# A one-core block of scans, long convolutions and expert retrieval: how the routing looks up the sixteen chosen keys of a pair

## The chip, the cores and the metric

The kernel runs on one core of a Trainium2 chip. The metric is the device time of one execution in microseconds (us). Engines are called as in the profile: PE multiplies matrices (PEld loads its weights), DVE, ACT and POOL are the vector, scalar and GpSimd engines, SP issues transfers.

## The reference

One trunk layer over 1024 latent tokens of width 1024, with a context of 256 tokens: an input projection, two parallel mixers (a state-space scan in both directions and a gated long convolution), an output projection, then a retrieval over 128 x 128 single-neuron experts. The change touches the retrieval only:

```python
q = (hb @ wq).reshape(PEER_BLOCK, PEER_HEADS, 2, PEER_DKEY // 2)
s = jnp.einsum('thsd,snd->thsn', q, subkeys).astype(jnp.float32)
s1, i1 = lax.top_k(s[:, :, 0], PEER_TOPK)
s2, i2 = lax.top_k(s[:, :, 1], PEER_TOPK)
cand = (s1[..., :, None] + s2[..., None, :]).reshape(PEER_BLOCK, PEER_HEADS, PEER_TOPK * PEER_TOPK)
sc, ci = lax.top_k(cand, PEER_TOPK)
e1 = jnp.take_along_axis(i1, ci // PEER_TOPK, axis=-1)
e2 = jnp.take_along_axis(i2, ci % PEER_TOPK, axis=-1)
idx = e1 * PEER_KEYS + e2
gate = jax.nn.softmax(sc, axis=-1).astype(hb.dtype)
```

For every token and each of 8 heads, the 16 best of 128 keys are found on either side, then the 16 best pairs. `take_along_axis` turns a pair's two ranks (0 to 15) into its two key numbers (0 to 127). The experts' rows are then weighted with the gates.

## The kernel before

The tokens lie in 8 blocks of 128, one token to a partition. Blocks 5 to 7 gather their experts' rows by number (class `Experts`, `gathered`: indirect transfers that POOL issues, L1511, with a DVE dot product, L1535, or a weighted sum, L1548, for each row). Blocks 0 to 4 are done densely: the scores of all 128 groups of 128 experts are computed by PE (`score`, L1634), multiplied by a table of gates, and sent through PE again (`down`, L1674). The dense table of gates comes from `Route.spread`.

Routing (`peer`, class `Route`) has these parts:

- `firsts`, `first`: PE multiplies the tokens with merged key matrices (`qacc`, L1368), ACT copies the scores out (`r_sc`, L1370), and DVE finds the top 16 of 128 by MAX8, FIND_INDEX8 and MATCH_REPLACE8 (`top16`, L1344 to L1348).
- `second(b)`, the function that changes: for one block it adds the candidate pairs (L1396, L1398), finds the top 16 of 112 for each head, splits the position of a pair into two ranks (L1410 to L1418), and looks the ranks up. The lookup is made twice, t = 0 and 1 for the two sides. A one-hot tile `r_oh` of 128 x (8 heads x 16 pairs x 16 ranks) is written by a comparison of each pair's rank with 0 to 15 (L1423), multiplied by the 16 key numbers of the head (L1425), and summed over ranks by one reduction (L1427). ACT makes the key numbers (`r_if`, L1393) for both sides in one 128x256 activation. Softmax of the gates follows (L1431 to L1436).
- `spread(b)`, for blocks 0 to 4: one-hot rows e0 and e2 by DVE (L1457, L1459), e0 times the gate split between POOL (three of eight tokens, L1461) and ACT (five, L1463), products by PE (L1467), copied out by ACT (L1469) and stored.

Which runs beside which is written in `peer` with the generators `both` and `chain`: `second(5)` beside the firsts of blocks 6 and 7, `second(6)` and `second(7)` beside the firsts of blocks 0 to 4, `second(0)` after these, and `second(b + 1)` beside `spread(b)`. At each step `Experts.beside` adds 48 score tiles in all and some of the gathered rows. How many of these are done before the last stage is counted in steps, not in time. Within this, a scheduler with a model of the engines sets the order of instructions on each engine. Every engine runs its own list in order.

The last stage (`pour`, `run`), after routing, works off the remaining scores, the down products and the remaining rows.

Of the kernel before, what the change touches and what calls it, by code (L numbers as in the profile page):

```python
# [12 lines left out]
BF16 = mybir.dt.bfloat16  # L13
I32 = mybir.dt.int32
U32 = mybir.dt.uint32
AF = mybir.ActivationFunctionType
ALU = mybir.AluOpType
AX = mybir.AxisListType
# [1272 lines left out]
class Route:  # L1291
# [9 lines left out]
    def tables(self, mid):  # L1301
        nc = self.K.nc
        it = mid.tile([128, 128], I32, name="iota_i")
        nc.gpsimd.iota(it, pattern=[[1, 128]], base=0, channel_multiplier=0)
        self.iota = mid.tile([128, 128], F32, name="iota_f")
        nc.vector.tensor_copy(self.iota, it)
        self.val = mid.tile([128, NB, 16, 16], F32, name="r_val")
        self.idx = mid.tile([128, NB, 16, 16], U32, name="r_idx")

# [76 lines left out]
    def second(self, b, wk):  # L1386


        K, nc = self.K, self.K.nc
        V = nc.vector  # L1390
        val = self.val[:, b]
        idf = wk.tile([128, 16, 16], BF16, name="r_if", bufs=1)
        nc.scalar.activation(idf, self.idx[:, b], AF.Copy)  # L1393
        cand = wk.tile([128, 8, 112], F32, name="r_cand", bufs=1)
        v1, v2 = val[:, 0:16:2], val[:, 1:16:2]
        V.tensor_add(cand[:, :, :64].rearrange("p h (i j) -> p h i j", j=16),  # L1396
                     v1[:, :, 0:4, None].to_broadcast([128, 8, 4, 16]), v2[:, :, None, :].to_broadcast([128, 8, 4, 16]))
        V.tensor_add(cand[:, :, 64:].rearrange("p h (i j) -> p h i j", j=4),  # L1398
                     v1[:, :, 4:16, None].to_broadcast([128, 8, 12, 4]), v2[:, :, None, 0:4].to_broadcast([128, 8, 12, 4]))
        s = wk.tile([128, 8, 16], F32, name="r_s", bufs=2)  # L1400
        ci = wk.tile([128, 8, 16], U32, name="r_ci", bufs=2)
        tmp2 = wk.tile([128, 112], F32, name="r_tmp2", bufs=2)
        for h in range(8):
            self.top16(s[:, h], ci[:, h], cand[:, h], tmp2)
            if h % 2:
                yield
        pos = wk.tile([128, 4, 8, 16], U32, name="r_pos", bufs=1)
        for j, (n, op) in enumerate(((4, ALU.logical_shift_right), (15, ALU.bitwise_and),
                                     (2, ALU.logical_shift_right), (3, ALU.bitwise_and))):
            V.tensor_scalar(pos[:, j], ci, n, None, op0=op)  # L1410
        pof = wk.tile([128, 4, 8, 16], F32, name="r_pof", bufs=1)
        nc.scalar.activation(pof, pos, AF.Copy)
        up = wk.tile([128, 8, 16], F32, name="r_up", bufs=1)
        V.tensor_scalar(up, pof[:, 0], 4.0, None, op0=ALU.is_ge)
        V.scalar_tensor_tensor(pof[:, 2], pof[:, 2], 12.0, pof[:, 0], op0=ALU.subtract, op1=ALU.subtract)
        V.tensor_sub(pof[:, 3], pof[:, 3], pof[:, 1])
        V.tensor_mul(pof[:, 2:4], pof[:, 2:4], up[:, None].to_broadcast([128, 2, 8, 16]))
        V.tensor_add(pof[:, 0:2], pof[:, 0:2], pof[:, 2:4])  # L1418
        e = wk.tile([128, 2, 8, 16], F32, name="r_e", bufs=2)
        for t in range(2):  # L1420
            oh = wk.tile([128, 8, 16, 16], BF16, name="r_oh", bufs=2)
            ohv = oh.rearrange("p h k j -> p (h k) j")
            V.tensor_tensor(ohv, pof[:, t].rearrange("p h k -> p (h k)")[:, :, None].to_broadcast([128, 128, 16]),  # L1423
                                    self.iota[:, None, :16].to_broadcast([128, 128, 16]), op=ALU.is_equal)
            V.tensor_mul(oh, oh, idf[:, t:16:2, None, :].to_broadcast([128, 8, 16, 16]))  # L1425
            yield
            V.tensor_reduce(e[:, t].rearrange("p h k -> p (h k)"), ohv, axis=AX.X, op=ALU.add)  # L1427
        ef = e.rearrange("p t h k -> p t (h k)")
        g = self.gate[b] if b >= ND else wk.tile([128, 128], F32, name="r_g", bufs=2)
        gv = g.rearrange("p (h k) -> p h k", k=16)  # L1430
        V.tensor_sub(gv, s, s[:, :, 0:1].to_broadcast([128, 8, 16]))  # L1431
        nc.scalar.activation(g, g, AF.Exp)
        sm = wk.tile([128, 8], F32, name="r_sm", bufs=1)
        V.tensor_reduce(sm, gv, axis=AX.X, op=ALU.add)
        V.reciprocal(sm, sm)
        V.tensor_mul(gv, gv, sm[:, :, None].to_broadcast([128, 8, 16]))  # L1436
        if b >= ND:
            V.scalar_tensor_tensor(self.ids[b], ef[:, 0], 128.0, ef[:, 1], op0=ALU.mult, op1=ALU.add)
        self.found = ef, g
# [484 lines left out]
```

## Time and profile before

| | |
|---|---|
| median of 3 runs | 4202.12 us (4198.15 to 4209.2) |
| the profiled execution's own time | 4209.43 us |
| its span | 4207.5 us |
| mean granted TensorE clock | 0.954 |
| routing, from the end of the output projection to the last stage | about 1795 to 2560 us of the span |

In the page's rows a group is a line, an engine and an operation with `out<-in`, the count, busy time and the mean ns of one. Rows of a view by tile give the shortest, the median and the longest duration instead. Rows of a timeline begin with the start and the duration in us. Busy time of an instruction includes the time that it stands still at an operand.

### The profile page before, as it was taken

Reading aid. Unit: us, or ns where it says so; the run is one execution under the profiler, and the core shown is the slowest. Engines: PE = TensorE matmul, PEld = TensorE weight load, DVE = VectorE, ACT = ScalarE, POOL = GpSimd, SP = SyncE. Lnnn points to the kernel's source line nnn. Section 1 sums busy time; section 2 is a strip of 40 time slices with the busy share of each in tenths; the row PEclk is TensorE's granted clock in tenths of the full one; section 3 lists DMA queues with packets and bytes.
Section 4 is the critical chain, followed back from the end, with each engine's and each line's share of the span. In section 5 each row is a group of like instructions: output and inputs, shape, how many; then the busy total and the mean of one; then the engine's idle time right before and its main releaser. Section 6 shows DMA issues by size and latency. Waiting matters only on the chain.

```text
span 4207.5 us, 60407 instructions
## 1 busy us (share of the span) xinstructions
PE 3807.4 (90%) x21993; PEld 3346.8 (80%) x21993; DVE 3385.1 (80%) x5997; ACT 1389.8 (33%) x2674; POOL 2045.4 (49%) x1643
## 2 busy tenths in 40 slices
PE   5999999898898997789999968899989999999996
PEld 3787887787888896689999867788878888788785
DVE  5665787546799795599999996788878889888798
ACT  3233333325563121242236664222222222222221
POOL 2232323344343121066435445666667776777675
PEclk8999999998899998899999999999999999999998
DMA  6333333466766446567546547899989999999897
GB/s 204 110 124 98 125 120 127 133 204 206 235 210 204 152 145 177 175 236 267 197 158 231 191 161 259 284 321 318 348 300 337 326 327 346 337 322 338 317 330 259
DMA packets 509673, 974.12 MB, mean 232 GB/s; under 512 B 33771, under 2 KB 291231, under 8 KB 506432
## 3 DMA queue, kind: packets, MB, share of 16 engines
q1 hardware_dynamic: 395616, 557.25, 40.4%
q0 software_dynamic: 110880, 405.98, 26.3%
q10 hardware_dynamic: 2880, 7.03, 0.5%
q8 instruction: 173, 2.83, 0.3%
q14 instruction: 124, 1.02, 0.1%
HBM read 823.20 MB, written 146.95 MB: 231 GB/s over the span
## 4 chain that ended last, share of the span: by engine, by line
PE 39%; DVE 22%; DMA 13%; issue 7%; POOL 6%; ACT 3%; SPq 1%; POOLq 0%; DVEq 0%; ACTq 0%
PE x_acc L1674 9%; PE x_s L1634 8%; PE mm L199 7%; DMA x_vr<-in_peer_v_dram 6%; POOL rows L1511 3%; DVE rows L1535 3%; PE pe L1134 2%; PE hy L850 2%; POOL x_vl L1606 2%; DVE r_e L1459 2%; PE tp L850 1%; DVE r_e L1457 1%; PE hx L850 1%; DMA s_e<-d_cum 1%; DMA rows<-in_peer_u_dram,ids 1%
## 5 line engine op out<-in xcount | busy, mean ns | idle before, releaser
L1634 PE MATMUL x_s<-fTh,x_uh 128*128 128x320 f32 x2048 | 642.9, 314 | 15.0 <-ACT x_a L1635 15.0
L1634 PE MATMUL x_s<-fTh,x_ul 128*128 128x320 f32 x2048 | 640.1, 313 | 5.5 <-DVE x_ul L1595 5.5
L1634 PE MATMUL x_s<-fTl,x_uh 128*128 128x320 f32 x2048 | 640.5, 313 | 0.0
L1674 PE MATMUL x_acc<-x_vl,x_ah 128*128 128x512 f32 x1280 | 517.2, 405 | 18.3 <-POOL x_vl L1606 18.3
L1674 PE MATMUL x_acc<-x_vh,x_ah 128*128 128x512 f32 x1280 | 451.9, 405 | 85.0 <-ACT x_vh L1605 61.4
L1548 DVE SCALAR_TENSOR_TENSOR e_p<-rows,e_a,e_p 128x1024 f32<-128x1024 f32 x381 | 489.6, 1285 | 35.1 <-DMA rows<-in_peer_v_dram,ids 27.6
L1674 PE MATMUL x_acc<-x_vh,x_al 128*128 128x512 f32 x1280 | 512.2, 402 | 0.0
L1511 POOL DMA_INDIRECT rows<-in_peer_u_dram,ids x384 | 417.7, 1088 | 177.7 <-DVE rows L1535 54.5
L1535 DVE SCALAR_TENSOR_TENSOR rows<-rows,e_p 128x1024 f32<-128x1024 f32 x384 | 456.2, 1210 | 34.1 <-DMA rows<-in_peer_u_dram,ids 33.7
L1511 POOL DMA_INDIRECT rows<-in_peer_v_dram,ids x384 | 402.8, 1049 | 133.1 <-issue 62.9
L1606 POOL TENSOR_TENSOR x_vl<-x_vr,x_vh 128x512 fp32r<-128x512 f32 x256 | 340.1, 1332 | 191.0 <-ACT x_vh L1605 187.6
L1634 PEld LDWEIGHTS x_s<-fTh,x_uh 128*128 128x128 f32 x2048 | 390.5, 191 | 30.1 <-ACT x_a L1635 19.9
L1634 PEld LDWEIGHTS x_s<-fTh,x_ul 128*128 128x128 f32 x2048 | 389.7, 190 | 15.5 <-DVE x_ul L1595 6.9
L1634 PEld LDWEIGHTS x_s<-fTl,x_uh 128*128 128x128 f32 x2048 | 390.4, 191 | 9.4
L1674 PEld LDWEIGHTS x_acc<-x_vh,x_ah 128*128 128x128 f32 x1280 | 242.1, 194 | 139.3 <-ACT x_vh L1605 69.3
L1674 PEld LDWEIGHTS x_acc<-x_vl,x_ah 128*128 128x128 f32 x1280 | 249.8, 195 | 72.0 <-POOL x_vl L1606 26.2
L1605 ACT ACTIVATE x_vh<-x_vr 128x512 fp32r<-128x512 f32 x256 | 160.0, 627 | 423.3 <-DMA x_vr<-in_peer_v_dram 349.6
L1674 PEld LDWEIGHTS x_acc<-x_vh,x_al 128*128 128x128 f32 x1280 | 249.0, 195 | 49.4
L1595 POOL TENSOR_TENSOR x_ul<-x_raw,x_uh 128x1024 fp32r<-128x1024 f32 x57 | 140.3, 2461 | 281.6 <-ACT x_uh L1594 281.3
L199 PE MATMUL mm<-xh,whi 128*128 128x512 f32 (+1 forms) x784 | 263.9, 412 | 7.4 <-DVE acc L235 3.6
L199 PE MATMUL mm<-xl,whi 128*128 128x512 f32 (+1 forms) x784 | 263.8, 411 | 7.1 <-DVE xl L51 7.1
L1594 ACT ACTIVATE x_uh<-x_raw 128x1024 fp32r<-128x1024 f32 x128 | 135.2, 1057 | 400.1 <-PE x_s L1634 355.4
(382 smaller groups left out, 8704.3 us busy)
## 6 DMA issues: line engine op xcount, KB each, us to landing
x_raw<-in_peer_uT_dram SPq DMA_DIRECT2D x128, 512.0 KB
x_vr<-in_peer_v_dram SPq DMA_DIRECT2D x256, 256.0 KB
d_G<-r_st SPq DMA_DIRECT2D x20, 2048.0 KB
x_g<-d_G SPq DMA_DIRECT2D x32, 1280.0 KB
wraw<-in_w_mod_dram SPq DMA_DIRECT2D x32, 1024.0 KB
wraw<-in_w_in_dram SPq DMA_DIRECT2D x24, 1024.0 KB
wk_w<-d_WK SPq DMA_DIRECT2D x24, 1024.0 KB
d_kr<-h_k SPq DMA_DIRECT2D x32, 512.0 KB
```

Source lines behind the costliest of these rows:

```text
L199: nc.tensor.matmul(p, w[:, k], x[j][:, k, t0:t0 + n], start=(k == 0 and q == 0), stop=(k == 7 and q == 2))
L850: nc.tensor.matmul(out, self.m[mats][:, tl, :], x, start=(n == 0), stop=(n == len(terms) - 1))
L1134: nc.tensor.matmul(p, a[:, k], w[:, ss], start=(k == 0 and q == 0), stop=(k == n - 1 and q == 2))
L1511: nc.gpsimd.indirect_dma_start(out=r, out_offset=None, in_=table, in_offset=bass.IndirectOffsetOnAxis(ap=ids[:, j:j + 1], axis=0))
L1535: nc.vector.scalar_tensor_tensor(r, r, 1.0, f, op0=ALU.mult, op1=ALU.mult, accum_out=d[:, j:j + 1])
L1548: nc.vector.scalar_tensor_tensor(acc, r, a[:, j:j + 1], acc, op0=ALU.mult, op1=ALU.add)
L1594: nc.scalar.activation(hi, raw, AF.Copy)
L1595: self.pace = (nc.vector if self.turn('u', UR if self.n < NE else UP) else nc.gpsimd).tensor_sub(lo, raw, hi.bitcast(F32)).ins
L1605: nc.scalar.activation(hi, raw, AF.Copy)
L1606: self.pace = nc.gpsimd.tensor_sub(lo, raw, hi.bitcast(F32)).ins
L1634: nc.tensor.matmul(s[:, :SW], w[:, k], x[:, k, ms], start=(k == 0 and q == 0), stop=(k == 7 and q == 2))
L1674: self.K.nc.tensor.matmul(p, a[x][:, bs], v[w], start=(m == 0 and q == 0), stop=(m == SC - 1 and q == 2))
```

## The change

The lookup works in 16-bit numbers throughout, and the one-hot tile has another layout. The ranks of the pairs are written as BF16 (`r_pob`). The tile `r_oh` now has, for each head, 16 ranks by 16 pairs, pairs innermost. The comparison is against a table `r_rank` that is made once. ACT writes the key numbers of one side expanded to 128x2048 (`r_if`, one buffer), once for each side, so that of the second side waits until the multiplication of the first has read the buffer. The reduction is replaced by four additions over halves: 128, 64, 32 and 16 elements for each head, the last one into the fp32 tile `r_e`.

```diff
+        self.rank = mid.tile([128, 16, 16], BF16, name="r_rank")
+        nc.vector.tensor_copy(self.rank, self.iota[:, :16, None].to_broadcast([128, 16, 16]))
...
-        idf = wk.tile([128, 16, 16], BF16, name="r_if", bufs=1)
-        nc.scalar.activation(idf, self.idx[:, b], AF.Copy)
...
-        V.tensor_add(pof[:, 0:2], pof[:, 0:2], pof[:, 2:4])
+        pob = wk.tile([128, 2, 8, 16], BF16, name="r_pob", bufs=1)
+        V.tensor_add(pob, pof[:, 0:2], pof[:, 2:4])
         e = wk.tile([128, 2, 8, 16], F32, name="r_e", bufs=2)
         for t in range(2):
+
+            key = wk.tile([128, 8, 16, 16], BF16, name="r_if", bufs=1)
+            nc.scalar.activation(key, self.idx[:, b, t:16:2, :, None].to_broadcast([128, 8, 16, 16]), AF.Copy)
             oh = wk.tile([128, 8, 16, 16], BF16, name="r_oh", bufs=2)
-            ohv = oh.rearrange("p h k j -> p (h k) j")
-            V.tensor_tensor(ohv, pof[:, t].rearrange("p h k -> p (h k)")[:, :, None].to_broadcast([128, 128, 16]),
-                                    self.iota[:, None, :16].to_broadcast([128, 128, 16]), op=ALU.is_equal)
-            V.tensor_mul(oh, oh, idf[:, t:16:2, None, :].to_broadcast([128, 8, 16, 16]))
+            V.tensor_tensor(oh, pob[:, t, :, None, :].to_broadcast([128, 8, 16, 16]),
+                            self.rank[:, None].to_broadcast([128, 8, 16, 16]), op=ALU.is_equal)
+            V.tensor_mul(oh, oh, key)
             yield
-            V.tensor_reduce(e[:, t].rearrange("p h k -> p (h k)"), ohv, axis=AX.X, op=ALU.add)
+            for n in (8, 4, 2):
+                V.tensor_add(oh[:, :, :n], oh[:, :, :n], oh[:, :, n:2 * n])
+            V.tensor_add(e[:, t], oh[:, :, 0], oh[:, :, 1])
```

DVE gets 49 instructions more in all (three for each of 16 half lookups, and the table), ACT eight more. The scheduler also sets other instructions of routing and of the last stage in a somewhat different order. Two places, in the order lists of the engines (line numbers behind the change are its own).

DVE, the lookup of block 5, before (`gTl` is the transposed activation of another block, `x_ul` the low part of an expert weight tile):

```order
L1418 TENSOR_TENSOR r_pof<-r_pof 128x256
L1423 TENSOR_TENSOR r_oh<-r_pof,iota_f 128x2048 x2
L51 TENSOR_TENSOR gTl<-qt,gTh 128x4x128
L1425 TENSOR_TENSOR r_oh<-r_oh,r_if 128x2048 x2
L1595 TENSOR_TENSOR x_ul<-x_raw,x_uh 128x1024
L1427 TENSOR_REDUCE r_e<-r_oh 128x128 x2
```

and with the change:

```order
L1419 TENSOR_TENSOR r_pob<-r_pof 128x256
L1426 TENSOR_TENSOR r_oh<-r_pob,r_rank 128x2048 x2
L1428 TENSOR_TENSOR r_oh<-r_oh,r_if 128x2048
L51 TENSOR_TENSOR gTl<-qt,gTh 128x4x128
L1431 TENSOR_TENSOR r_oh<-r_oh 128x8x128
L1431 TENSOR_TENSOR r_oh<-r_oh 128x8x64
L1431 TENSOR_TENSOR r_oh<-r_oh 128x8x32
L1428 TENSOR_TENSOR r_oh<-r_oh,r_if 128x2048
L1432 TENSOR_TENSOR r_e<-r_oh 128x128
L1600 TENSOR_TENSOR x_ul<-x_raw,x_uh 128x1024
```

The second multiplication has moved behind three of the first side's additions; between the two multiplications ACT expands the second side's keys.

DVE, the lookup of block 4, the last one, beside the spreading of block 3, before:

```order
L1457 TENSOR_TENSOR r_e_21429<-iota_f,r_T 128x1024
L1418 TENSOR_TENSOR r_pof<-r_pof 128x256
L1423 TENSOR_TENSOR r_oh<-r_pof,iota_f 128x2048 x2
L1425 TENSOR_TENSOR r_oh<-r_oh,r_if 128x2048 x2
L1427 TENSOR_REDUCE r_e<-r_oh 128x128 x2
L1457 TENSOR_TENSOR r_e_21468<-iota_f,r_T 128x1024
```

and with the change (from the comparison to the second multiplication and the two instructions behind it):

```order
L1426 TENSOR_TENSOR r_oh<-r_pob,r_rank 128x2048 x2
L1464 TENSOR_TENSOR r_e_21105<-iota_f,r_T 128x1024
L1462 TENSOR_TENSOR r_e_21103<-iota_f,r_T 128x1024
L1428 TENSOR_TENSOR r_oh<-r_oh,r_if 128x2048
L1462 TENSOR_TENSOR r_e_21126<-iota_f,r_T 128x1024
L1464 TENSOR_TENSOR r_e_21128<-iota_f,r_T 128x1024
L1431 TENSOR_TENSOR r_oh<-r_oh 128x8x128
L1464 TENSOR_TENSOR r_e_21224<-iota_f,r_T 128x1024
L1462 TENSOR_TENSOR r_e_21222<-iota_f,r_T 128x1024
L1428 TENSOR_TENSOR r_oh<-r_oh,r_if 128x2048
L1431 TENSOR_TENSOR r_oh<-r_oh 128x8x64
L1464 TENSOR_TENSOR r_e_21250<-iota_f,r_T 128x1024
```

The six instructions of this lookup stood in one piece; now the one-hot rows of the spreading stand between them, four of these between the two multiplications.

## Rows read from the trace of the kernel before

**Rows 1.** The page, busy time by engine.
```profile
PE 3807.4 (90%) x21993; PEld 3346.8 (80%) x21993; DVE 3385.1 (80%) x5997; ACT 1389.8 (33%) x2674; POOL 2045.4 (49%) x1643
```

**Rows 2.** The chain that ended last, from 1795 to 2560 us, by line.
```profile
by line: DVE rows L1535 10.9%; PE x_s L1634 8.7%; DVE r_e L1459 8.3%; DVE r_e L1457 7.9%; issue 7.2%; PE qg L1467 4.9%; DVE r_tmp L1346 4.7%; DVE r_oh L1423 4.2%; POOL r_e L1461 4.1%; PE qacc L1368 3.2%; DVE r_idx L1348 3.2%; DVE r_idx L134
```

**Rows 3.** Windows of routing: start and end, us, busy us of each engine, clock, DMA.
```profile
1795.00:2100.00 305.00, 284.02 (x2059) 279.99 (x2060) 296.46 (x1101) 94.81 (x140) 171.07 (x98) 0.95 0.67 240
2100.00:2175.00 75.00, 74.10 (x553) 73.58 (x552) 74.38 (x355) 21.59 (x38) 24.09 (x14) 1.00 0.35 116
2175.00:2505.00 330.00, 286.80 (x2104) 276.69 (x2102) 326.75 (x496) 216.02 (x537) 157.38 (x102) 0.98 0.56 207
2505.00:2560.00 55.00, 37.49 (x277) 34.54 (x276) 48.04 (x38) 41.44 (x113) 24.33 (x16) 0.92 0.33 136
...
sum 765.00, PE 682.42 PEld 664.79 DVE 745.62 ACT 373.87 POOL 376.88; mean PE 170.60 PEld 166.20 DVE 186.41 ACT 93.47 POOL 94.22
```

**Rows 4.** The one-hot tile: shortest, median and longest duration, ns.
```profile
L1423 DVE TENSOR_TENSOR r_oh<-r_pof,iota_f x16: 2270/2279/6702, 1816.2 to 2495.4; 128x2048 bf16<-128x2048 f32 x16
L1425 DVE TENSOR_TENSOR r_oh<-r_oh,r_if x16: 1200/1213/2287, 1825.6 to 2498.8; 128x2048 bf16<-128x2048 bf16 x16
L1427 DVE TENSOR_REDUCE r_e<-r_oh x16: 2261/2271/2281, 1829.0 to 2502.1; 128x128 f32<-128x2048 bf16 x16
```

**Rows 5.** The ranks' tile, the same view.
```profile
L1415 DVE SCALAR_TENSOR_TENSOR r_pof<-r_pof x8: 271/278/2487, 1812.6 to 2487.2; 128x128 f32<-128x128 f32 x8
L1416 DVE TENSOR_TENSOR r_pof<-r_pof x8: 277/279/285, 1812.8 to 2487.4; 128x128 f32<-128x128 f32 x8
L1417 DVE TENSOR_TENSOR r_pof<-r_pof,r_up x8: 402/414/1045, 1813.1 to 2489.9; 128x256 f32<-128x256 f32 x8
L1418 DVE TENSOR_TENSOR r_pof<-r_pof x8: 399/730/3099, 1813.6 to 2492.3; 128x256 f32<-128x256 f32 x8
```

**Rows 6.** The candidates, the same view.
```profile
L1396 DVE TENSOR_TENSOR r_cand<-r_val x8: 669/720/3729, 1796.1 to 2384.7; 128x512 f32<-128x512 f32 x8
```

**Rows 7.** DVE groups from 1790 to 2560 us: busy us, mean ns.
```profile
L1423 DVE TENSOR_TENSOR r_oh<-r_pof,iota_f 128x2048 bf16<-128x2048 f32 x16 | 42.7, 2707 | 0.1
L1427 DVE TENSOR_REDUCE r_e<-r_oh 128x128 f32<-128x2048 bf16 x16 | 36.0, 2272 | 0.0
...
L1425 DVE TENSOR_TENSOR r_oh<-r_oh,r_if 128x2048 bf16<-128x2048 bf16 x16 | 22.5, 1424 | 0.0
...
L1396 DVE TENSOR_TENSOR r_cand<-r_val 128x512 f32<-128x512 f32 x8 | 11.1, 1390 | 0.0
L1418 DVE TENSOR_TENSOR r_pof<-r_pof 128x256 f32<-128x256 f32 x8 | 9.4, 1178 | 0.0
...
L1415 DVE SCALAR_TENSOR_TENSOR r_pof<-r_pof 128x128 f32<-128x128 f32 x8 | 4.4, 554 | 0.0
L1417 DVE TENSOR_TENSOR r_pof<-r_pof,r_up 128x256 f32<-128x256 f32 x8 | 3.9, 490 | 0.0
```

**Rows 8.** DVE timeline at the lookup of block 5: start, duration.
```profile
1816.21 8.91 DVE L1423 TENSOR_TENSOR r_oh<-r_pof,iota_f 128x2048 bf16<-128x2048 f32 x2
...
1829.05 4.46 DVE L1427 TENSOR_REDUCE r_e<-r_oh 128x128 f32<-128x2048 bf16 x2
```

**Rows 9.** POOL timeline at the same place.
```profile
1817.02 5.96 POOL L51 TENSOR_TENSOR wk_l<-wk_w,wk_h 128x2048 fp32r<-128x2048 f32 x1 [1.12 <-ACT wk_h L50]
1830.33 4.62 POOL L51 TENSOR_TENSOR wk_l<-wk_w,wk_h 128x2048 fp32r<-128x2048 f32 x1 [7.36 <-ACT wk_h L50]
```

**Rows 10.** ACT groups from 1790 to 2560 us.
```profile
L50 ACT ACTIVATE wk_h<-wk_w 128x2048 fp32r<-128x2048 f32 x16 | 30.6, 1910 | 13.1 <-PE qacc L1368 13.0
...
L1393 ACT ACTIVATE r_if<-r_idx 128x256 bf16<-128x256 uint32 x8 | 3.3, 414 | 16.0 <-DVE r_idx L1348 8.3 <-DVE r_oh L1425 7.7
```

**Rows 11.** The cast behind the table of 0 to 127.
```profile
L1306 DVE CAST iota_f<-iota_i x1: 220/220/220, 1656.3 to 1656.3; 128x128 f32<-128x128 int32 x1
```

**Rows 12.** What PE waited for from 2175 to 2510 us: us, times, longest.
```profile
PE qt L1447 <- DVE r_e L1427: 9.0, 1, 9.0
```

## Prediction

> **What bounds the kernel now.** On the page no engine has more than PE's 90% and DVE's 80% [rows 1], but that is a mean over stages. The lookup runs only in routing, so I read that stretch alone. In its windows DVE is busy 745.6 of 765 us, and 98% of the first three [rows 3]: 5 of 8 lookups fall into the first two of these, 3 into the third. The chain by line agrees: most of its named shares are DVE lines, and the comparison L1423 alone has 4.2% of 765 us, some 32 us [rows 2]. So a DVE microsecond saved here is near to one saved in all. It doesn't hold everywhere. From 2100 to 2175 us PE is busy 74.1 of 75 us [rows 3]; one lookup (block 0) lies there. And from 2505 us on PE, POOL and DVE run in step, with no lookup left.
>
> The last stage is not reached by the change except through the scheduler's order; the work that is done ahead of it is counted in steps, so it inherits the same rest.
>
> **The change, part by part.** All durations are of the profiled execution.
>
> *Comparison.* 16 instructions with a median of 2.279 us, with an fp32 operand pair [rows 4]. The new one has three 16-bit operands over the same 2048 elements, laid as in the multiplication L1425 (16-bit, a broadcast middle axis), whose median is 1.213 us [rows 4]. That is the price I take: 1.07 us saved in each half lookup.
>
> *Multiplication.* Same size and type as before, 1.213 us; nothing.
>
> *Reduction against the tree.* The reduction takes 2.271 us [rows 4]. The four additions have 1024, 512, 256 and 128 elements. For their prices I draw a line through the rows: at one element a step, 512 elements take 0.669 us and 2048 take 2.270, so 1.04 ns each and 0.135 us fixed [rows 4, 6]; at the rate of L1425, (1.213 - 0.135) / 2048 = 0.53 ns each. The first three additions then take 0.67, 0.40 and 0.27 us, and the last, with an fp32 output, 0.28 as L1416 with as many elements [rows 5]. Sum 1.62 us, saved 0.65. The other end is one element a step for all: 1.20 + 0.67 + 0.40 + 0.28 = 2.55 us, a loss of 0.28.
>
> Both together: 1.07 + 0.65 = 1.72 us in each of 16 halves, **27.5 us** of DVE (12.6 at the other end).
>
> *Ranks and table.* `r_pob` costs what L1418 cost. The table is one copy of 256 elements, twice L1306's 0.22 us at most [rows 11], beside the output projection: nothing.
>
> *What the additions meet.* This is the uncertain term. DVE's instructions with two operands in SBUF are often stretched: L1423 reaches 6.702 us and L1418 3.099 against 0.399 [rows 4, 5]. The reduction, with one operand, never leaves 2.261 to 2.281 us in 16 cases [rows 4]. The timelines show what stretches them. In block 5, POOL's subtraction starts behind the first L1423, and the pair of L1423 takes 8.91 us, about 4.4 more than two medians; the next such subtraction of 4.62 us runs right through the two reductions, and neither side is longer for it [rows 8, 9]. So a reduction is a time in which POOL works for free; the tree is four more places at which DVE may stand behind POOL. The nearest row is L1425: same tile, same place, same type. Its excess over 16 medians is 22.5 - 19.4 = 3.1 us, 0.19 each [rows 4, 7]. The chain L1415 to L1418 is nearer in shape (four short, dependent instructions): its three stretched members have 17.7 us against 8 x 1.072 = 8.6 of their shortest, so 9.1 us over 32 instructions, 0.28 each [rows 5, 7]. The far end is L1396, (11.1 - 5.4) / 8 = 0.72 each [rows 6, 7]. The near end is 0, if an addition only waits where the next two-operand instruction would have. I take 0.19, because the place decides what POOL is doing: 64 x 0.19 = **12.2 us given back** (0 to 46). The stretch of the comparison itself, 42.7 - 36.5 = 6.2 us [rows 4, 7], I leave as it is.
>
> On this a rule of the Trainium skill speaks against the change: "SBUF — State Buffer", section "Who interferes with whom", says that a DVE instruction with two SBUF inputs contends with a GpSimd instruction that reads SBUF, and that a reduction never does. The trace agrees with both halves of it. By the rule alone, the 36.0 us of reductions stop being free, and with POOL busy 376.9 of 765 us 17.7 us would go, which leaves 9.8 instead of 15.3; the time by it, 4195 us, lies within the forecast's own stretch.
>
> *Keys on ACT.* Before, 8 activations of 0.414 us; now 16 of 2048 elements, for which L50's 1.910 us stands [rows 10]: 30.6 - 3.3 = 27.3 us more on ACT. ACT is busy 374 of 765 us [rows 3], so the amount has room. What matters is the order: the second side's keys have one buffer and wait for the first multiplication, and the second multiplication waits for them. In block 5 only `gTl` and three additions stand between, 0.67 + 1.34 = 2.0 us, against 1.91 and two hand-overs: a fraction of a microsecond. In block 4 four one-hot rows stand there, over 4 us, and in the others as many. Behind the waiting activation on ACT's list stand the copies of the score tiles and, in the third window, `r_st`; PE waits for both. I count **1 us**; if nothing covered it, it would be 8 x 1.91 = 15.3 us.
>
> *The last lookup.* Before, it stood in one piece, and PE waited 9.0 us for the last reduction [rows 12]. Now block 3's one-hot rows stand between, so PE is fed meanwhile, but DVE has the same amount to do before the last addition. The gain is in the sum already; I add nothing.
>
> *Block 0.* Its two halves lie where PE is full: their 2 x (1.72 - 0.76) = 1.9 us I count as nothing.
>
> Sum: 27.5 - 12.2 - 1 - 1.9 = 12.4, rounded to **12 us**. The profiled execution took 4209.4 us (span 4207.5), so this one would take 4197.4. It stood 7.3 above the median of 4202.1; against the median the forecast is **4190 us**.
>
> **The rivals.**
>
> *A. All of DVE's saving comes out.* POOL's instructions are as many as before; one that meets an addition no longer meets the next one-hot row. Then 27.5 us, and up to 6 more if the shorter comparison is stretched less: 4175 to 4168 us. For it: no idle DVE time to lose it in. Against: 4.62 us of POOL under one pair of reductions.
>
> *B. The faster rate doesn't come.* If the comparison runs at 2.28 us or the additions, which read and write rows of a strided tile, at one element a step, the saving falls by 15 to 17 us, and the stalls eat the rest: about 4202 us. Against: L1425 has nearly the same patterns. The change then doesn't do what it says.
>
> *C. Slower: the tree stands behind POOL.* If each addition pays as L1396 does, 0.72 us, 64 cost 46 us against 27.5 saved: 18 us slower, 4220. It decides from 0.43 us for each addition. For it: L1418 is not far, 0.78 a piece (9.4 - 3.2 over 8). Against: L1416, in the same chain, is never stretched, longest 0.285 us [rows 5], so neighbours share one stall.
>
> *D. PE binds instead.* PE is busy 93% of the first window and 87% of the third [rows 3]. If its waits don't shrink, half of the 12 us goes, and the new order of the last stage adds or takes some: 4196 to 4206 us.
>
> **How the numbers follow.** A difference of 0.3% is 12.6 us, below 4189.5 or above 4214.7. The forecast (4183 to 4197) gets 0.42 and lies across that line, 0.20 of it faster. A gets 0.20, faster. B gets 0.10, no change, and D 0.15, 0.13 of it no change and 0.02 faster; C gets 0.10, slower; 0.03 is left for an order of the last stage that costs more than 12 us. Faster is 0.20 + 0.20 + 0.02 = 0.42, the same 0.22 + 0.10 + 0.13 = 0.45, slower 0.13. The range reaches from A's first end to the near part of C: 4172 to 4210.
>
> **What would show it.** The comparison at 1.2 us and the tree at some 1.6 us a half, in groups by line; the mean of the first addition against its shortest gives the stall. DVE's busy time from 1795 us to the last lookup should fall by 10 to 15 us, and the last stage should start some 12 us earlier. A DVE wait for ACT at the second multiplication of over 1 us, eight times, would show the keys uncovered. The prediction is wrong if the additions are stretched by over 0.4 us on average, if they run at one element a step, or if the start of the last stage moves and the end doesn't.

## The result and the profile after

| | before | after |
|---|---|---|
| median of 6 runs each, first batch | 4200.17 us | 4183.28 us (4178.73 to 4193.91) |
| ratio, with its 95% interval | | 0.995 [0.9932, 0.9969] |
| a later batch (11 and 6 runs) | 4207.67 us | 4190.66 us (4183.98 to 4204.3) |
| ratio, with its 95% interval | | 0.9964 [0.995, 0.9978] |
| profiled execution, first batch | 4209.43 us, span 4207.5 | 4193.91 us, span 4192.0 |

The change makes the kernel 17 us faster, both times; the forecast was 12 (4190 us, with a range of 4172 to 4210) and rival A 27.5 or more. That is 0.4 to 0.5%, and both intervals are clear of no change.

The page of after, busy time by engine. DVE lost 30 us, ACT gained 23 [rows 1].

```profile
PE 3802.2 (91%) x21993; PEld 3339.3 (80%) x21993; DVE 3355.2 (80%) x6046; ACT 1412.6 (34%) x2682; POOL 2038.9 (49%) x1643
```

To compare routing as a whole I take it from the last `o_f` of L1268, at the end of the output projection, to the last store of the table of gates (`d_G`). One window of before, then the windows of after (start and end, length, busy us of PE, PEld, DVE, ACT and POOL, clock, DMA share, GB/s).

```profile
1793.60:2558.10 764.50, 680.52 (x4973) 662.89 (x4974) 746.99 (x1989) 373.94 (x828) 376.88 (x229) 0.97 0.57 206
```

```profile
1797.40:2100.00 302.60, 283.82 (x2100) 280.47 (x2101) 292.71 (x1190) 106.06 (x145) 169.87 (x94) 0.97 0.66 232
2100.00:2175.00 75.00, 74.69 (x542) 74.17 (x542) 73.38 (x311) 28.93 (x49) 26.13 (x18) 1.00 0.46 155
2175.00:2490.00 315.00, 283.88 (x2089) 273.35 (x2087) 313.97 (x507) 226.67 (x543) 155.57 (x102) 0.99 0.56 209
2490.00:2539.10 49.10, 34.12 (x246) 32.02 (x247) 39.86 (x33) 36.91 (x101) 23.93 (x17) 0.90 0.47 193
sum 741.70, PE 676.51 PEld 660.02 DVE 719.92 ACT 398.57 POOL 375.51; mean PE 169.13 PEld 165.00 DVE 179.98 ACT 99.64 POOL 93.88
```

Routing went from 764.5 to 741.7 us, 22.8 less. DVE's busy time in it went from 747.0 to 719.9, 27.1 less, and its idle time from 17.5 to 21.8. The other engines have what they had, but for ACT's keys.

The one-hot tile of after: shortest, median and longest duration in ns. These answer to [rows 4]: the comparison runs at 1.224 us instead of 2.279.

```profile
L1431 DVE TENSOR_TENSOR r_oh<-r_oh x48: 265/417/3256, 1828.4 to 2473.9; 128x1024 bf16<-128x1024 bf16 x16, 128x512 bf16<-128x512 bf16 x16, 128x256 bf16<-128x256 bf16 x16
L1426 DVE TENSOR_TENSOR r_oh<-r_pob,r_rank x16: 1209/1224/5620, 1820.0 to 2450.4; 128x2048 bf16<-128x2048 bf16 x16
L1428 DVE TENSOR_TENSOR r_oh<-r_oh,r_if x16: 1203/1220/3411, 1826.6 to 2461.3; 128x2048 bf16<-128x2048 bf16 x16
L1432 DVE TENSOR_TENSOR r_e<-r_oh x16: 260/282/2299, 1831.0 to 2475.2; 128x128 f32<-128x128 bf16 x16
```

DVE groups of after, 1790 to 2560 us: busy us, mean ns. These answer to [rows 7].

```profile
L1428 DVE TENSOR_TENSOR r_oh<-r_oh,r_if 128x2048 bf16<-128x2048 bf16 x16 | 25.7, 1607 | 0.1
L1426 DVE TENSOR_TENSOR r_oh<-r_pob,r_rank 128x2048 bf16<-128x2048 bf16 x16 | 24.6, 1582 | 0.0
L1431 DVE TENSOR_TENSOR r_oh<-r_oh 128x1024 bf16<-128x1024 bf16 x16 | 12.7, 796 | 0.0
L1431 DVE TENSOR_TENSOR r_oh<-r_oh 128x512 bf16<-128x512 bf16 x16 | 9.8, 613 | 0.0
L1432 DVE TENSOR_TENSOR r_e<-r_oh 128x128 f32<-128x128 bf16 x16 | 9.7, 606 | 0.0
L1396 DVE TENSOR_TENSOR r_cand<-r_val 128x512 f32<-128x512 f32 x8 | 8.9, 1108 | 0.0
L1431 DVE TENSOR_TENSOR r_oh<-r_oh 128x256 bf16<-128x256 bf16 x16 | 8.7, 544 | 0.1
L1419 DVE TENSOR_TENSOR r_pob<-r_pof 128x256 bf16<-128x256 f32 x8 | 6.1, 764 | 0.0
...
L1417 DVE TENSOR_TENSOR r_pof<-r_pof,r_up 128x256 f32<-128x256 f32 x8 | 3.9, 482 | 0.1
...
L1415 DVE SCALAR_TENSOR_TENSOR r_pof<-r_pof 128x128 f32<-128x128 f32 x8 | 2.3, 285 | 0.0
```

The four additions sum to 12.7 + 9.8 + 8.7 + 9.7 = 40.9 us, more than the 36.0 us of the reductions that they replace. At their unhindered lengths (0.68, 0.41, 0.28 and 0.28, 1.64 us a half before rounding) they would take 26.3; so 14.6 us are stretch, 0.23 each. The comparison fell from 42.7 to 24.6. The comparison, the multiplication and the sum together went from 101.2 to 91.2 us, so only 10 of the 27 us show in the sums of the lookup's own rows. Another 3.7 are overlap, which such sums count twice. In the records a DVE instruction starts about 0.08 us before the one in front of it has ended: the two reductions of [rows 8] take 4.46 us together, not 2 x 2.271, and in after an addition ends at 2005.43 + 0.27 = 2005.70, with the next instruction begun at 2005.62.

```profile
2005.43 0.27 DVE L1431 TENSOR_TENSOR r_oh<-r_oh 128x256 bf16<-128x256 bf16 x1
2005.62 1.21 DVE L1540 SCALAR_TENSOR_TENSOR rows<-rows,e_p 128x1024 f32<-128x1024 f32 x1
```

With 48 instructions more, 48 x 0.08 = 3.7 us of their durations cost no busy time. The remaining 13 us lie in instructions that the change does not shorten. The candidates L1396 went from 11.1 to 8.9, the last step of the ranks (L1418, now L1419) from 9.4 to 6.1 and L1415 from 4.4 to 2.3 [rows 7]; all three are among the rows that were stretched before [rows 5, 6]. The one-hot rows of the spreading fell by 6.2 us, in before

```profile
L1457 DVE TENSOR_TENSOR r_e<-iota_f,r_T 128x1024 f32<-128x1024 f32 x80 | 125.1, 1567 | 2.8 <-ACT r_T L1449 2.8
L1459 DVE TENSOR_TENSOR r_e<-iota_f,r_T 128x1024 f32<-128x1024 f32 x80 | 110.8, 1394 | 0.4 <-PE qg L1467 0.4
```

and in after:

```profile
L1462 DVE TENSOR_TENSOR r_e<-iota_f,r_T 128x1024 f32<-128x1024 f32 x80 | 116.2, 1454 | 0.0
L1464 DVE TENSOR_TENSOR r_e<-iota_f,r_T 128x1024 f32<-128x1024 f32 x80 | 113.5, 1423 | 0.0
```

Other rows grew, `x_ul` from 33.2 to 36.0 us among them.

What stretches an addition is seen in two timelines of after (start, duration). First three additions on DVE, then POOL at the same places.

```profile
2002.72 0.41 DVE L1431 TENSOR_TENSOR r_oh<-r_oh 128x512 bf16<-128x512 bf16 x1
...
2008.41 2.36 DVE L1431 TENSOR_TENSOR r_oh<-r_oh 128x512 bf16<-128x512 bf16 x1
...
2070.64 3.26 DVE L1431 TENSOR_TENSOR r_oh<-r_oh 128x256 bf16<-128x256 bf16 x1
```

```profile
2001.56 1.79 POOL L1516 DMA_INDIRECT rows<-in_peer_u_dram,ids  x1 [0.30 <-DVE r_val L1349]
...
2008.05 2.42 POOL L1600 TENSOR_TENSOR x_ul<-x_raw,x_uh 128x1024 fp32r<-128x1024 f32 x1
...
2069.10 4.64 POOL L51 TENSOR_TENSOR wk_l<-wk_w,wk_h 128x2048 fp32r<-128x2048 f32 x1 [6.29 <-ACT wk_h L50]
```

The addition of 512 elements takes 0.41 us beside POOL's issue of a gather, and 2.36 beside a POOL subtraction of 2.42, until that ends. One of 256 elements takes 3.26, until the subtraction of 4.64 ends. Of the 64 additions, 13 are longer by over 0.15 us (14.6 us in all), and each of them starts while a POOL instruction with two operands is running; 17 overlap gather issues alone, and none of these is longer; eight meet a two-operand instruction of POOL that starts after them, and are not longer either. The Trainium skill's "SBUF — State Buffer", section "Who interferes with whom", says that a DVE instruction with two SBUF inputs contends with a GpSimd instruction that reads SBUF; the trace agrees, with 0.41 against 2.36 us.

### The profile page after: what moved, and what is told of

Read it like the earlier page. It is cut to its first block, busy times and chain, and to the rows that moved or that the text cites. A ratio compares the mean times of both kernels' runs of the same rounds, so it can differ in the third digit from the quotient of the medians.

```text
span 4192.0 us, 60480 instructions
## 1 busy us (share of the span) xinstructions
PE 3802.2 (91%) x21993; PEld 3339.3 (80%) x21993; DVE 3355.2 (80%) x6046; ACT 1412.6 (34%) x2682; POOL 2038.9 (49%) x1643
## 5 line engine op out<-in xcount | busy, mean ns | idle before, releaser
L1639 PE MATMUL x_s<-fTh,x_uh 128*128 128x320 f32 x2048 | 641.7, 313 | 10.6 <-ACT x_a L1640 10.4
L199 PE MATMUL mm<-xh,wlo 128*128 128x512 f32 (+1 forms) x784 | 264.8, 413 | 0.4 <-POOL wlo L51 0.4
```

Of the source, the lines that this page charges most:

```text
L199: nc.tensor.matmul(p, w[:, k], x[j][:, k, t0:t0 + n], start=(k == 0 and q == 0), stop=(k == 7 and q == 2))
L1639: nc.tensor.matmul(s[:, :SW], w[:, k], x[:, k, ms], start=(k == 0 and q == 0), stop=(k == 7 and q == 2))
```

## The experiments

Before's median was 4205.55 us in the batch of the first four, 4202.32 in that of the next four, 4203.9 in that of the three after, 4207.67 in the last. A column of the table gives the difference to the median in the same batch. DVE's busy time and the length of routing are of the profiled execution, as above.

| run | time less before, us | ratio, interval | DVE busy | routing |
|---|---|---|---|---|
| before | | | 747.0 | 764.5 |
| after, first | -16.9 | 0.995 [0.9932, 0.9969] | 719.9 | 741.7 |
| after, again | -17.0 | 0.9964 [0.995, 0.9978] | 720.3 | 742.8 |
| one strided reduction | +13.3 | 1.0032 [1.0018, 1.0046] | 757.6 | 782.2 |
| one addition, strided reduction | -5.6 | 0.9985 [0.9974, 0.9995] | 736.9 | 758.8 |
| tree alone | +15.8 | 1.0038 [1.0024, 1.0052] | 745.6 | 763.7 |
| fp32 comparison | +10.7 | 1.0025 [1.0011, 1.0039] | 742.7 | 767.6 |
| comparison alone | +1.5 | 1.0 [0.9989, 1.001] | 726.5 | 753.9 |
| two key buffers | -19.6 | 0.995 [0.9933, 0.9967] | 726.7 | 750.3 |
| before, POOL relieved | -15.1 | 0.9959 [0.9944, 0.9973] | 726.3 | 747.0 |
| after, POOL relieved | -28.2 | 0.9928 [0.9912, 0.9945] | 704.1 | 732.0 |
| joint tree | -25.9 | 0.9941 [0.9922, 0.996] | 714.2 | 736.9 |
| joint tree, two key buffers | -1.0 | 1.0002 [0.9991, 1.0014] | 720.3 | 750.6 |
| keys by side | +4.0 | 1.0011 [0.9999, 1.0022] | 742.1 | 762.6 |

**One reduction in the new layout.** The changed kernel with its four additions replaced:

```diff
-            for n in (8, 4, 2):
-                V.tensor_add(oh[:, :, :n], oh[:, :, :n], oh[:, :, n:2 * n])
-            V.tensor_add(e[:, t], oh[:, :, 0], oh[:, :, 1])
+            V.tensor_reduce(e[:, t], oh.rearrange("p h r k -> p h k r"), axis=AX.X, op=ALU.add)
```

> The change with the tree replaced by one reduction over ranks again (16 reductions over a strided view of the new tile); comparison, keys and table stay as in the change. Theory 'port' (an addition with two operands in SBUF stands behind POOL's instructions, a reduction does not): the tree cost 40.5 us of DVE in all, 16 reductions of 2.27 us cost 36.3, none stretched; 4 us faster than the change, 4179 us, at most the same. Rival 'rate' (only the instructions' own lengths count, the stalls go elsewhere anyhow): 16 x 0.65 us slower than the change, 4194 us.

Its reduction against the one of before:

```profile
L1430 DVE TENSOR_REDUCE r_e<-r_oh x16: 3895/4056/4312, 1827.3 to 2512.9; 128x128 f32<-128x2048 bf16 x16
```

With 16 elements between the numbers that it sums, the reduction takes 4.056 us, not 2.271 [rows 4]. So the run doesn't price the tree against a reduction of before. Its 16 sum to 65.5 us, 24.6 more than the tree of after, most of its distance of some 30 us to after. Neither theory had this price. The run does show that in this layout one reduction is no substitute for the tree.

**One addition, then a reduction over 8.**

```diff
-            for n in (8, 4, 2):
-                V.tensor_add(oh[:, :, :n], oh[:, :, :n], oh[:, :, n:2 * n])
-            V.tensor_add(e[:, t], oh[:, :, 0], oh[:, :, 1])
+            V.tensor_add(oh[:, :, :8], oh[:, :, :8], oh[:, :, 8:])
+            V.tensor_reduce(e[:, t], oh[:, :, :8].rearrange("p h r k -> p h k r"), axis=AX.X, op=ALU.add)
```

> The change with one addition (128 elements of each head) and then one reduction over the remaining 8 ranks instead of four additions. Own lengths 0.67 + 1.20 us a half against 1.62. Theory 'port': 16 stretched instructions instead of 64, 30 + 4 us against the tree's 40.5, 4 to 7 us faster than the change, 4176 to 4179 us. Rival 'rate': 16 x 0.25 us = 4 us slower, 4187 us.

```profile
L1431 DVE TENSOR_REDUCE r_e<-r_oh x16: 2002/2110/2243, 1823.1 to 2478.3; 128x128 f32<-128x1024 bf16 x16
```

The strided price again, half of it for half of the elements. The run ends between after and the one before it, as its DVE time does.

**The tree alone**, in the old layout, behind the fp32 comparison.

```diff
-            V.tensor_reduce(e[:, t].rearrange("p h k -> p (h k)"), ohv, axis=AX.X, op=ALU.add)
+            for n in (8, 4, 2):
+                V.tensor_add(oh[:, :, :, :n], oh[:, :, :, :n], oh[:, :, :, n:2 * n])
+            V.tensor_add(e[:, t], oh[:, :, :, 0], oh[:, :, :, 1])
```

> The kernel before with only the reduction replaced by four additions over halves in the old layout; comparison in fp32 and keys as before. Theory 'port': 64 additions take some 26 us of their own and 10 to 18 us of standing behind POOL, against 36.0 us of reductions; the same as before, 4195 to 4206 us. Rival 'rate': 10 us faster than before, 4190 us.

```profile
L1428 DVE TENSOR_TENSOR r_oh<-r_oh x48: 369/458/4548, 1828.5 to 2500.0; 128x1024 bf16<-128x1024 bf16 x16, 128x512 bf16<-128x512 bf16 x16, 128x256 bf16<-128x256 bf16 x16
L1429 DVE TENSOR_TENSOR r_e<-r_oh x16: 370/406/1026, 1835.8 to 2502.3; 128x128 f32<-128x128 bf16 x16
```

The additions take 15.8 + 10.9 + 8.7 + 6.5 = 41.9 us for 36.0 of reductions, yet DVE's busy time in routing falls by 1.4: other rows are shorter here too. Routing is as long as before, the time 16 us longer, more than either theory allowed. The tree alone is no gain. It is not quite the tree of the change, either: in the old layout the smaller additions are slower, the last one 0.406 us by the median against 0.282 in after, and a half takes about 1.95 us of its own, not 1.64.

**The fp32 comparison**: the changed kernel with ranks and table in fp32, all else kept.

```diff
-        self.rank = mid.tile([128, 16, 16], BF16, name="r_rank")
+        self.rank = mid.tile([128, 16, 16], F32, name="r_rank")
...
-        pob = wk.tile([128, 2, 8, 16], BF16, name="r_pob", bufs=1)
+        pob = wk.tile([128, 2, 8, 16], F32, name="r_pob", bufs=1)
```

> The change with the ranks and the rank table in fp32, so that the comparison takes 2.28 us again; tree, layout and expanded keys stay. Theory 'comparison': 17 us slower than the change, no different from before, ratio 0.998 to 1.002. Rival 'tree' or 'order' (the gain comes from the tree, or from the new order in which the last lookup is interleaved with block 3's one-hot rows): at most 10 us slower than the change, ratio 0.9975 or below.

```profile
L1426 DVE TENSOR_TENSOR r_oh<-r_pob,r_rank x16: 2264/2278/6690, 1818.1 to 2476.2; 128x2048 bf16<-128x2048 f32 x16
```

The comparison is back at 2.278 us and 41.5 us in all, 16.9 more than in after; DVE's time in routing is 22.8 more, the run some 28 us slower than after, where 17 was expected. Without the 16-bit comparison the rest of the change is a loss.

**The comparison alone**: before with 16-bit ranks, spread out by ACT so that the old layout and its reduction can stay (16 more activations of 2048 elements).

```diff
-            V.tensor_tensor(ohv, pof[:, t].rearrange("p h k -> p (h k)")[:, :, None].to_broadcast([128, 128, 16]),
-                                    self.iota[:, None, :16].to_broadcast([128, 128, 16]), op=ALU.is_equal)
+            pw = wk.tile([128, 128, 16], BF16, name="r_pw", bufs=2)
+            nc.scalar.activation(pw, pof[:, t].rearrange("p h k -> p (h k)")[:, :, None].to_broadcast([128, 128, 16]), AF.Copy)
+            V.tensor_tensor(ohv, pw, self.rank[:, None].to_broadcast([128, 128, 16]), op=ALU.is_equal)
```

> The kernel before with the comparison alone in 16 bits: ACT expands the ranks to 128x2048 (16 activations of 1.9 us), layout, keys, multiplication and the one reduction over contiguous ranks stay. Theory 'comparison' (the change's gain is the comparison's 16 x 1.07 us, the tree gives its own back to standing behind POOL): 17 to 21 us faster than before, ratio 0.995 to 0.996, as fast as the change or up to 4 us faster. Rival 'tree' (the tree brings a part of its own 10 us): slower than the change by 5 us or more, ratio 0.997 or above. If the ranks' expansion is waited for, a DVE wait for ACT at the comparison shows it.

```profile
L1427 DVE TENSOR_TENSOR r_oh<-r_pw,r_rank x16: 1195/1216/3409, 1824.4 to 2465.3; 128x2048 bf16<-128x2048 bf16 x16
L1428 DVE TENSOR_TENSOR r_oh<-r_oh,r_if x16: 1195/1214/5249, 1827.8 to 2469.8; 128x2048 bf16<-128x2048 bf16 x16
L1430 DVE TENSOR_REDUCE r_e<-r_oh x16: 2255/2270/2279, 1830.1 to 2475.6; 128x128 f32<-128x2048 bf16 x16
```

The lookup takes 89.5 us here, as little as in after, and DVE's busy time falls by 20.5. But routing falls by 10.6 only and the time not at all. DVE now waits 13.9 us for gathered rows (2.0 before) and 3.2 for POOL:

```profile
DVE rows L1538 <- DMA rows<-in_peer_u_dram,ids: 13.9, 8, 4.1
...
DVE r_e L1460 <- POOL r_e L1464: 3.2, 2, 1.7
```

Both theories had expected a gain here. So the parts are not additive in time: the tree with its keys and layout costs 11 us (fp32 comparison), the comparison alone gives nothing, and both together give 17. In DVE's busy time they nearly add up: -4.3 and -20.5, against -27.1 for both. Each of these kernels has an order of its own, which is part of every one of these figures.

**Two key buffers**: `r_if` with `bufs=2` in the changed kernel.

> The change with two buffers for the expanded keys, so that the second side's keys no longer wait for the first multiplication. Theory 'covered': DVE never waited for these keys; ACT's wait for DVE's multiplication (25.4 us, 12 times) goes, the time stays within 3 us of the change, 4180 to 4186 us. Rival 'keys' (what stands behind the waiting activation on ACT, score tiles and the copies of products, holds PE up): 8 us or more faster, 4175 us.

In after, ACT waits 25.4 us for the multiplication that frees the buffer, but DVE waits for its keys only 0.1 us (row L1428 of the groups). With two buffers ACT's wait is 17.9, where it was expected to go:

```profile
ACT r_if L1424 <- DVE r_oh L1428: 25.4, 12, 6.5
```

```profile
ACT r_if L1424 <- DVE r_oh L1428: 17.9, 6, 10.9
```

The ratio is the same. The keys are covered. But the same instructions in this order keep DVE busy for 726.7 us of routing, 6.8 more than in after:

```profile
1795.10:2545.40 750.30, 681.60 (x4973) 666.65 (x4974) 726.73 (x2037) 400.65 (x837) 380.52 (x229) 0.96 0.58 210
```

**POOL relieved**, in both kernels: `wk_l` is not subtracted by POOL; ACT writes a second rounded copy in its place. The kernels leave out that subtraction, so the scores differ.

```diff
-        self.K.split(w, hi, lo, KP)
+        self.K.nc.scalar.activation(hi, w, AF.Copy)
+        self.K.nc.scalar.activation(lo, w, AF.Copy)
```

> The kernel before without POOL's subtraction of the key matrices: the low part is a second ACT copy of the raw tile, so the scores that choose the experts are others (the same number of everything). 77 us of POOL go, 31 us are added on ACT. For comparison with the next kernel, and for the stretch of two-operand instructions from 1795 to 2175 us: theory 'port' says that L1423's and L1418's longest (6.7 and 3.1 us) fall to below 4 us; rival 'not POOL': they stay. Time: some 10 us faster than before.

> The change without POOL's subtraction of the key matrices, in the same way (the low part is a second ACT copy). Theory 'port': the additions' mean stretch up to 2175 us falls to below 0.1 us each, the tree's 40.5 us to below 36, and the gap to the kernel before without that subtraction grows from 17 us to 20 or more. Rival 'not POOL': the additions stay at 40 us and the gap at 17 us or below.

Without POOL's longest subtractions before gains 15 us and after 11, so the two stand 13 us apart, not further than with them. DVE's busy time falls by 22.2 between the two (27.1 with POOL's work). If the tree paid more for these subtractions than the reductions did, the distance should have grown; that theory fell. In the relieved kernel before, the pair of comparisons in block 5 is no longer stretched (2.29 and 2.28 us), where one took 6.702 [rows 4]: there POOL's subtraction had held it up. The longest comparison still takes 4.48. In the relieved kernel after, the four additions still take 15.9 + 11.6 + 5.3 + 6.3 = 39.1 us, not the 36 or less that were expected: what remains of POOL's two-operand work stretches them nearly as much.

**Joint tree**: both sides in one tile, one tree for both, 32 additions of twice the size.

```diff
+        both = wk.tile([128, 2, 8, 16, 16], BF16, name="r_oh", bufs=1)
         for t in range(2):
...
-            oh = wk.tile([128, 8, 16, 16], BF16, name="r_oh", bufs=2)
+            oh = both[:, t]
...
-            for n in (8, 4, 2):
-                V.tensor_add(oh[:, :, :n], oh[:, :, :n], oh[:, :, n:2 * n])
-            V.tensor_add(e[:, t], oh[:, :, 0], oh[:, :, 1])
+        oh = both.rearrange("p t h j k -> p (t h) j k")
+        for n in (8, 4, 2):
+            V.tensor_add(oh[:, :, :n], oh[:, :, :n], oh[:, :, n:2 * n])
+        V.tensor_add(e.rearrange("p t h k -> p (t h) k"), oh[:, :, 0], oh[:, :, 1])
```

> The changed kernel, but both sides lie in one tile and the tree runs once over both: 32 additions of twice the size in place of 64. Own length by the rows of the changed kernel's smaller ones: the largest 1.21 (as the multiplication), then 0.67, 0.41, 0.41 us, 2.7 for a block against 3.2, so 4 us less of DVE in all. Theory 'a stall for each addition' (0.23 us each): 32 fewer give another 7 us, the tree's rows sum to about 29 us and the time is about 4172. Theory 'the stall belongs to POOL's instruction': the additions that stretch stand to the end of one subtraction of POOL, so halving their number saves nothing beyond the own length: tree about 36 us, time about 4179. Rival 'the scheduler's order decides': over 4186 or under 4168, with the difference in waits or outside of routing.

```profile
L1433 DVE TENSOR_TENSOR r_oh<-r_oh 128x2048 bf16<-128x2048 bf16 x8 | 12.4, 1544 | 0.0
...
L1433 DVE TENSOR_TENSOR r_oh<-r_oh 128x1024 bf16<-128x1024 bf16 x8 | 8.9, 1117 | 0.0
...
L1433 DVE TENSOR_TENSOR r_oh<-r_oh 128x512 bf16<-128x512 bf16 x8 | 5.5, 691 | 0.0
...
L1434 DVE TENSOR_TENSOR r_e<-r_oh 128x256 f32<-128x256 bf16 x8 | 4.5, 567 | 0.0
```

The tree takes 31.3 us: 21.7 of its own and 9.6 of stretch (14.6 in after). The stretch on the tree fell by 5.0, nearer to the theory of a stall for each addition. But DVE's busy time in routing fell by 5.7 only, of which own length is 4.6 by the durations, or some 2 when the overlaps of 32 instructions are taken off. So between 1 and 4 us of the stretch that the tree lost came out, and as another order alone moves DVE's busy time by more than that (two key buffers, keys by side), the run does not decide between the theories. This is the fastest median of the kernels that leave nothing out; its interval overlaps with both of after's, so it is not told apart from after.

**Joint tree with two key buffers.**

> As the run with one tree for both sides, with two buffers for the keys, so that the second multiplication does not wait for ACT behind the first. Theory 'durations decide': the same as that run within 4 us, since the keys were covered. Theory 'the order alone is worth some microseconds': over 5 us apart.

Nothing was expected of a second buffer, and the run is 25 us slower than the one with one buffer. DVE's busy time in routing is 6 us more. Its wait for gathered rows, the first line here, is 17.6 us in 13 places; with one buffer, the second, it was 6.9 in 7:

```profile
DVE rows L1542 <- DMA rows<-in_peer_u_dram,ids: 17.6, 13, 4.8
```

```profile
DVE rows L1542 <- DMA rows<-in_peer_u_dram,ids: 6.9, 7, 1.4
```

Routing is 13.7 us longer, and what follows it 1659.0 us against 1645.7, the longest of all 14 profiles. The buffer changes no unhindered duration of the lookup; it changes the order that the scheduler sets.

**Keys by side**: before with only its keys split in two activations of 128 elements.

```diff
-        idf = wk.tile([128, 16, 16], BF16, name="r_if", bufs=1)
-        nc.scalar.activation(idf, self.idx[:, b], AF.Copy)
...
+            key = wk.tile([128, 8, 16], BF16, name="r_if", bufs=1)
+            nc.scalar.activation(key, self.idx[:, b, t:16:2], AF.Copy)
```

> The kernel before, with only the keys made one side at a time (16 activations of 128 elements in one buffer for 8 of 256). DVE has the same instructions with the same lengths, ACT about 2 us more, and the scheduler sets another order. Theory 'durations decide': 4202 to 4206, within 0.1% of before. Theory 'the order alone is worth some microseconds': over 5 us away from before, to either side, with DVE's busy time in routing the same within 4 us and the difference in its waits.

Another order at the same durations: 4 us slower by the medians, with an interval that reaches to no change. DVE's wait for gathered rows is 7.7 us here (2.0 before). So a reordering can be harmless, and can cost 25 us as above. DVE's busy time is 4.9 us less than in before, more than the 4 that was expected, though the instructions and their unhindered lengths are the same: less stretch, by order alone.

```profile
1788.50:2551.10 762.60, 678.05 (x4973) 664.36 (x4974) 742.11 (x1989) 376.70 (x835) 387.81 (x229) 0.96 0.57 206
```

**After, again.**

> The changed kernel once more, unchanged, for a second profiled execution and a narrower interval. Theory 'routing is fixed by the program, what lies around it varies from execution to execution': routing again 742 us long within 2, with DVE busy 720 within 2, while its start (1797.4 before) and the rest behind it (1652.9) move by several us. Rival 'the length of the last stage belongs to the program's order': start and rest the same within 2 us as well. The time 4180 to 4187 either way.

The two executions of after, the same window of each (start, end and columns as above); the second:

```profile
1794.40:2537.20 742.80, 681.39 (x4973) 666.52 (x4974) 720.25 (x2037) 399.38 (x837) 377.50 (x229) 0.96 0.59 212
```

Routing 742.8 us against 741.7, DVE 720.3 against 719.9: routing belongs to the program. What lies around it does not repeat so well: before its start 1794.4 against 1797.4 us, behind its end 1648.1 against 1652.9, together 8 us. The median of 4190.7 us lies above the 4180 to 4187 that was expected, as before's does in this batch.

## Why the prediction was right, and where it was wrong

- **The bound.** DVE was said to set the pace of routing, and a microsecond of it to be near one in all. DVE's busy time fell by 27.1 us, routing by 22.8, the time by 17. In all 14 profiles routing is DVE's busy time plus 17 to 30 us of idle. One reading was off, and nothing hangs on it: four lookups, not five, lie in the first two windows (comparisons from 1816, 1989, 2060 and 2157 us), and four in the third.
- **Comparison.** Predicted 1.213 us, measured 1.224. The fp32 run shows that there is no gain without this term, the comparison alone that it is not enough by itself in time. Rival B is out.
- **Own length of the tree.** Predicted 0.67 + 0.40 + 0.27 + 0.28; the additions that nothing hinders have 0.68, 0.41, 0.28 and 0.28. By these durations own lengths fell by 26.9 us, near the 27.5 of the prediction. What the prediction left out is the overlap of neighbours: in busy time, 48 instructions more take off 3.7, so 30.6 us.
- **What the additions meet: the term that was mis-sized.** The stretch on the tree was sized well, 0.23 us each against 0.19, and its cause was right. What was wrong in after is to count all of it as "12.2 us given back". 30.6 us came off own lengths and 27.1 off DVE's busy time, so some 3.5 were given back: 14.6 us of stretch came onto the tree, but the ranks, the candidate rows and the one-hot rows lost most of that amount. That is in part the mechanism of rival A, which I gave 0.20. It is not a law of this kernel. Own length less the fall of DVE's busy time is 30.6 - 20.3 = 10.3 us with two key buffers, 30.6 - 22.2 = 8.4 between the two kernels with POOL relieved, 13.7 - 4.3 = 9.4 in the fp32 run (the tree's part of the 30.6) and 8.8 - 1.4 = 7.4 in the tree alone, while the comparison alone gains 3.5 more than its own 17.0. And before itself has 4.9 us of stretch that another order takes away (keys by side); against that kernel after gives back 8.4. So how much of the stretch is a net cost depends on the order, from 3.5 to some 10 us here; that it moves from row to row is shown in after's rows, what decides how much does is not. Of the rule of the Trainium skill ("SBUF — State Buffer", section "Who interferes with whom") the trace bears out the contention of single instructions. The 17.7 us that I worked out from it as a loss did not come in any of these kernels.
- **What took its place.** Rival A's first end was all 27.5 us out of the time. In after DVE's idle time in routing grew by 4.3 us: 30.6 - 3.5 - 4.3 = 22.8, routing's own figure. The wait that grew is that for gathered rows, which the prediction did not name (2.0 before):

```profile
DVE rows L1540 <- DMA rows<-in_peer_u_dram,ids: 10.2, 7, 5.5
```

DVE comes to these rows sooner; that their transfers come no sooner is my reading of it, not tested.
- **Keys.** 1 us was counted; DVE waited 0.1. Block 0's 1.9 us were not tested by themselves.
- **PE.** Rival D's waits did not come: PE's idle time in routing fell from 84.0 to 65.2 us. PE's wait for the last addition fell from 9.0 us [rows 12] to 4.7:

```profile
PE qt L1452 <- DVE r_e L1432: 4.7, 3, 2.9
```

- **The last stage** starts 19.0 us earlier (last store of gates at 2539.1 us, before 2558.1), 20.9 in the second execution; 12 was forecast.
- **Rival C** is out by its own test: the additions pay 0.23 us, below the 0.43 from which it decides.
- **Luck in the sum.** The forecast of 12 is near 17 in part because errors of both signs met: own lengths 3.1 too low, the stretch 8.7 too high, waits and block 0 put at 2.9 where 4.3 came, and 5.8 between routing and the time that were not foreseen.

What stays open: routing is 22 us shorter and the time 17. With 8 us of scatter around routing between two executions of one kernel the profiles cannot place the other 5. Nor do they place it in three of the runs (tree alone, comparison alone, joint tree with two buffers), whose times are 12 to 17 us longer than routing's change says; for the others the two agree within 8. A profile is one execution, and before has only one: it took 4209.4 us, 4 to 7 above its median in these batches, while the tree alone was profiled 9 below its own median and the comparison alone 3 below, which makes up 13 of the 17 and 10 of the 12 us. In the joint tree with two key buffers the stage behind routing is longer, by 10 us against before; why that order costs it was not found. So the order is not excluded as a part of the 17: of the four kernels that have all of the shorter instructions and leave nothing out, three are 17 to 26 us faster than before, and this one is 1.

## What to carry to other kernels

When a bound engine shares stalls with another engine's instructions, a stretch that appears on new rows is not all a new cost: part of it may have left other rows. Read the net from the busy time of the bound engine as a whole, against own lengths with the overlap of neighbours taken off, and forecast it as a range; here 14.6 us on the new rows cost 3.5 net in one order, and 10 in another. Shorten the busy time of the bound engine and look next at what comes late for it, here the gathered rows. Where a scheduler sets the order, run the same durations in another order before a part is credited with 10 us: one buffer more moved this kernel by 25.

## What the runs showed of the hardware

- A 16-bit reduction over numbers that stand 16 elements apart took 4.056 us for 2048 elements and 2.110 for 1024; over adjacent ones it took 2.271 for 2048 [rows 4].
- A DVE addition of 0.28 us took 3.26 beside a POOL subtraction of 4.64, ending just behind it, while POOL's gather issues of 0.9 to 2.0 us stretched no addition of after. All 13 additions that were stretched began while a two-operand instruction of POOL was running; eight that began before one were not.
- The adjacent reduction stayed at 2.255 to 2.279 us in the run with the comparison alone, as before.
